# A two-layer hybrid transformer block: modulation weights in buffers of their own, a third pair begun early, bank copies asked for ahead of splits

## The chip, the cores and the metric

The kernel runs on one core of one Trainium2 chip. The core has a matrix engine (TensorE, PE in the profile; PEld is its loading of stationary operands), VectorE (DVE), ScalarE (ACT), GpSimd (POOL) and SyncE (SP). In this kernel SP starts nearly every load and store, in one queue. The engines run side by side and wait for each other by semaphores. The metric is the time of one execution on the device, in microseconds (us); lower is better.

## The reference

The reference is two layers over 1024 latent tokens and 256 context tokens, of width 1024, in 32-bit floats. Cut to what matters here:

```
def layer(x, ctx, c, c_ctx, ...):
    sh1, sc1, gt1, sh2, sc2, gt2 = split(silu(c) @ w_ada + b_ada, 6)      # modulation; the same for c_ctx
    px = (rms_norm(x, g1) * (1 + sc1) + sh1) @ w_in                       # q, k, v, f, u, gv
    mix = concat(latent_attention(q, k_all, v_all),                       # q, k: normed, rotary factors
                 fourier_mix(f), chunk_spatial_gate(u, gv)) @ w_out
    x = x + gt1 * mix
    y = rms_norm(x, g2) * (1 + sc2) + sh2
    x = x + gt2 * (square(relu(y @ w1)) @ w2)                             # w1: 1024 x 4096, w2: 4096 x 1024
```

The context tokens go through the same weights in layer 0 only, where layer 1's keys and values still need them; the output is x.

## The kernel before, in words

**Precision.** Each 32-bit operand is split into a high part, rounded by a copy on ScalarE, and the remainder, subtracted on VectorE. A product is three matmuls: high by high, high by low, low by high. So every weight block that is multiplied first passes ScalarE and VectorE.

**Stages of a layer.** Input projection, gMLP, Fourier mixing, attention in blocks of 128 queries, output mix (`mix_out`: product with `w_out`, gated residual L1323, sums of squares), second norm, MLP1, MLP2. The first 512 tokens' mix is done early, between attention units; the second 512 tokens' mix is the loop over `d` behind `split_next`, and the norm of the first half (`norm_first`) is stepped inside it.

**MLP1.** The hidden width is cut into 32 blocks of 128 columns, taken as 16 pairs `p`. Tokens (first and second 512), depth (first and second 512) and the two blocks of a pair make a 2 x 2 by 2 x 2 product, and it is done with seven products in place of eight, numbered 1 to 7, each of 12 matmuls of 128x512. In layer 0 four context products of 12 matmuls of 128x256 stand between them. The token sides (`ysum`) come from `norm_first` for products 2 and 4, and from `norm_second` for 5, 1, 7, 3, 6: the scaled x (L1464, L1465), sums (L1476, on GpSimd for c in (1, 3)), splits (L1470 on ScalarE, L1471 on VectorE). The weight sides come from `split_next`: a sum or difference of two raw blocks (L1576, in an M buffer; on GpSimd for products 2, 1, 6 in layer 0 and 2, 6 in layer 1, else on VectorE), the high part (L1578, ScalarE), the low part (L1580, VectorE), in a ring W1 of 8 buffers, that is, 4 splits. The matmuls are L1641 to L1643 (context) and L1655 to L1657.

**Behind a product.** `after_product` is called one product later. Products 2 and 4 of a pair share a PSUM bank, 5 and 3 another, 1 and 7 a third. After 2, 5 and 1 ScalarE copies the bank out (L1671). GpSimd adds copies 2 and 5 (L1673) and subtracts after product 1 (L1675); VectorE does the sums L1681, L1684, L1687 and L1691; ScalarE squares the relu (L1626, L1627); `combine` (L1618) makes five sums of the squared blocks, two of them on GpSimd, and they are stored for MLP2.

**The order of the work.** `seq` lists the products: the products 2 of pairs 0 and 1, then 4 and context for each, then 5, 1, 7, 3, 6 alternating between the two pairs, then pair after pair. `ahead_of` says how many steps of `norm_second` come ahead of a product; `split_next` is called until three splits lie ahead of the product's own, and only then are the matmuls and the pending `after_product` written. A scheduler reorders the instructions further within their dependences and buffers, so that the order on an engine isn't the code's. Buffers of one ring are given out in the order of first writing.

**Modulation.** `silu(c) @ w_ada` is a product of one vector, done on VectorE in most places. A unit (`ada_sums`, L317) is 256 columns of one of the six groups. Per step it loads 2 row blocks (256 KB) and at once multiplies each by its factor and adds it to a running sum in an SBUF buffer named pB (L328 for the first, L330 for the rest; the name pB is also that of the PSUM banks). A unit with `nj` = 2 does it for c and c_ctx: 16 instructions; with `nj` = 1 it has 8. Column sums on TensorE close it (L338, `ada_cols`). Layer 1's 20 units, 8 with `nj` = 2 and 12 with 1, load into the four M buffers that the raw sums use too, and are stepped once behind each product from pair 2 on in layer 0's MLP1, and what is left in MLP2. Layer 0's own first five units load 4 row blocks at a time into L buffers and are stepped every second step of the gMLP and projection (`GPUMP` = 2); `rope_tables` scales the rotary factors of both layers on VectorE (L636).

**MLP2** uses the same seven products with stored sums: 112 items of 12 matmuls, each with a load, a GpSimd sum of two weight blocks (L1738) and two splits (L1731, L1732; L1740, L1742), made two items ahead.

Of the kernel before, what the change touches and what calls it, by code (L numbers as in the profile page):

```python
# [11 lines left out]
F32 = mybir.dt.float32  # L12
# [27 lines left out]
GPUMP = 2  # L40
# [22 lines left out]
NBUF = {"S": 40, "L": 12, "T": 8, "M": 4, "R": 3, "W1": 8, "W2": 8, "pB": 5}  # L63
# [66 lines left out]
def hybrid_block_kernel(ctx: ExitStack, tc: tile.TileContext, a: dict, out: bass.AP):  # L130
# [186 lines left out]
    def ada_sums(l, c0, nj, mk, per):  # L317

        ac = [alloc("pB", [256], F32) for _ in range(nj)]
        for k0 in range(0, KC, per):  # L320
            w = mk(per, 256)
            load(w, a["w_ada"][l, k0 * P:(k0 + per) * P, c0:c0 + 256].rearrange("(k p) n -> p k n", p=P))
            for kk in range(per):
# [7 lines left out]
            yield None  # L331
        yield ac

    def ada_cols(l, grp, quarter, ac):
        tp = PB(2, 2)
        for j, x in enumerate(ac):
            for i in range(2):
                E.matmul(tp[:, j, i:i + 1], x[:, i * P:(i + 1) * P], ones[:, 0:1], start=True, stop=True)  # L338
        mod_cols(l, grp, quarter * 2, 2, [tp[:, j, :] for j in range(len(ac))])

    def ada_units(l, units, mk, per=4):

        prev = None
        for grp, quarter, nj in units:
            for ac in ada_sums(l, grp * D + quarter * 256, nj, mk, per):
                if ac is None:
                    yield
            if prev is not None:
                ada_cols(l, *prev)
                yield  # L350
            prev = grp, quarter, ac
        yield
        yield
        ada_cols(l, *prev)
        yield
# [261 lines left out]
    def layer(l, ys, norms, bank):  # L617
# [10 lines left out]
        def rope_tables():  # L628
# [7 lines left out]
            V.tensor_scalar_mul(grow[:, 0:4:2, :], grow[:, 0:4:2, :], -0.125)  # L636
# [842 lines left out]
        def norm_first():  # L1479

            if last:
                for k in range(KC):
                    to_tokens(0, k)
                    yield
# [3 lines left out]
            for k in range(KC):  # L1488
                x = modulated(0, res[0], k)
# [46 lines left out]
        def w1_load(p, which):  # L1536

            src = w1d[:, (p + NP * which) * P:(p + NP * which + 1) * P].rearrange("(k p) f -> p k f", p=P)
            if p % 2 and which:
                for half in range(2):  # L1540
                    t = alloc("W2", [4, P], F32)
                    load(t, src[:, 4 * half:4 * half + 4, :])
                    raws[p, which, half] = flat(t)
            else:
# [8 lines left out]
                "21": ((1, 0),), "12": ((0, 1),), "11": ((0, 0),)}  # L1553
# [453 lines left out]
```

## Time and profile before

| | |
|---|---|
| median of 3 runs | 2751.97 us (2745.11 to 2752.44) |
| the profiled execution | 2750.48 us, its span 2748.7 us |
| mean granted TensorE clock | 0.985 |
| loads of modulation weights into M | 80, of 256 KB, 3.1 us from issue to landing in the median |
| raw weight loads of MLP1 (R) | 48, of 512 KB, 4.3 us |
| VectorE's splits of weights in MLP1 (L1580, W from M) | 160, 149.6 us busy, 936 ns in the mean |
| their high parts (L1578, W from M) | 160, 98.2 us busy, 615 ns in the mean |
| idle time of ScalarE ahead of these high parts | 136.4 us, 54.8 of it for a raw sum on GpSimd |

How to read it: the profile is one execution. A row of the table by stage gives a stretch of the span in us, its length, and then for each engine the busy time with the number of instructions in brackets, the granted TensorE clock (1.00 is full speed), the share of the DMA engines and what they moved. A row of the groups gives line, engine, operation, output from inputs, shape and count, then busy us and mean ns, then the idle time just before them with what ended it. A row of the waits gives what waited for what: us in all, times, the longest. In the timeline, the first number is the start and the second the duration. Matmuls overlap, so that the busy time of one is longer than the step from one to the next.

### The profile page before, as it was taken

Reading aid. Unit: us, or ns where it says so; the run is one execution under the profiler, and the core shown is the slowest. Engines: PE = TensorE matmul, PEld = TensorE weight load, DVE = VectorE, ACT = ScalarE, POOL = GpSimd, SP = SyncE. Lnnn points to the kernel's source line nnn. Section 1 sums busy time; section 2 is a strip of 40 time slices with the busy share of each in tenths; the row PEclk is TensorE's granted clock in tenths of the full one; section 3 lists DMA queues with packets and bytes.
Section 4 is the critical chain, followed back from the end, with each engine's and each line's share of the span. In section 5 each row is a group of like instructions: output and inputs, shape, how many; then the busy total and the mean of one; then the engine's idle time right before and its main releaser. Section 6 shows DMA issues by size and latency. Waiting matters only on the chain. (4 is left out here: it accounts for less than half of the span.)

```text
span 2748.7 us, 39495 instructions
## 1 busy us (share of the span) xinstructions
PE 2613.8 (95%) x13236; PEld 2141.9 (78%) x13236; DVE 2129.4 (77%) x3663; ACT 1523.6 (55%) x3247; POOL 1064.0 (39%) x818
## 2 busy tenths in 40 slices
PE   7898899999899999999999999999999899999999
PEld 5677687787777777878878988787887688888877
DVE  7887979768898878865578684878677987766598
ACT  6535888666544334444455533889775555555443
POOL 4221745511443433334433000534314554424386
PEclk8999999999999999999999999999999999999999
DMA  8435221325054555695638521421252444486454
GB/s 280 143 110 156 79 95 36 115 70 186 29 186 159 171 159 168 212 323 169 197 118 294 163 81 57 129 92 33 88 166 87 134 157 150 164 281 202 138 170 144
DMA packets 314220, 405.08 MB, mean 147 GB/s; under 512 B 23816, under 2 KB 202400, under 8 KB 314016
## 3 DMA queue, kind: packets, MB, share of 16 engines
q1 hardware_dynamic: 308864, 393.38, 44.0%
q0 software_dynamic: 5152, 9.18, 1.2%
q8 instruction: 104, 1.70, 0.3%
q14 instruction: 100, 0.82, 0.1%
HBM read 298.92 MB, written 103.55 MB: 146 GB/s over the span
## 5 line engine op out<-in xcount | busy, mean ns | idle before, releaser
L1732 DVE TENSOR_TENSOR T<-R,T 128x512 fp32r<-128x512 f32 x224 | 186.8, 835 | 168.5 <-ACT T L1731 168.4
L1731 ACT CAST T<-R 128x512 fp32r<-128x512 f32 x224 | 138.9, 622 | 288.1 <-PE pB L197 269.7
L1142 DVE TENSOR_TENSOR T<-pB,T 128x512 fp32r<-128x512 f32 x328 | 223.3, 685 | 52.7 <-ACT T L1141 48.8
L1141 ACT CAST T<-pB 128x512 fp32r<-128x512 f32 x328 | 195.2, 600 | 72.9 <-PE pB L1139 37.2
L1655 PE MATMUL pB<-S,W 128*128 128x512 f32 x512 | 205.6, 402 | 5.6 <-ACT W L1671 3.7
L1657 PE MATMUL pB<-S,W 128*128 128x512 f32 x512 | 204.0, 398 | 4.4 <-DVE W L1580 4.1
L1656 PE MATMUL pB<-S,W 128*128 128x512 f32 x512 | 203.5, 397 | 2.3 <-DVE S L1471 2.3
L1106 DVE TENSOR_REDUCE mb<-pB 128x1 f32<-128x512 f32 x256 | 172.5, 683 | 35.4 <-PE pB L1061 34.2
L1738 POOL TENSOR_TENSOR M<-W,S 128x512 f32<-128x512 f32 x96 | 142.4, 1488 | 134.6 <-DVE W L1742 76.9
L1618 POOL TENSOR_TENSOR W<-T,T 128x512 f32<-128x512 f32 x64 | 110.5, 1746 | 185.9 <-ACT T L1627 185.9
L1122 ACT ACTIVATE L<-pB,nm 128x512 f32<-128x512 f32 x256 | 178.7, 704 | 0.1
L197 PE MATMUL pB<-W,T 128*128 128x512 f32 x448 | 175.5, 392 | 2.8 <-DVE W L1742 2.8
L196 PE MATMUL pB<-T,W 128*128 128x512 f32 x448 | 175.2, 391 | 2.3 <-ACT T L1731 2.3
L197 PE MATMUL pB<-T,W 128*128 128x512 f32 x448 | 174.8, 390 | 2.2 <-DVE T L1732 2.2
L198 PE MATMUL pB<-T,W 128*128 128x512 f32 x448 | 175.5, 392 | 1.3 <-DVE W L1742 1.1
L1139 PE MATMUL pB<-ident,L 128*128 128x128 f32 x1056 | 163.3, 277 | 14.0 <-DVE T L1142 6.4
L198 PE MATMUL pB<-W,T 128*128 128x512 f32 x448 | 174.5, 390 | 1.2 <-DVE T L1732 1.2
L196 PE MATMUL pB<-W,T 128*128 128x512 f32 x448 | 174.4, 389 | 0.0
L1578 ACT CAST W<-M 128x512 fp32r<-128x512 f32 x160 | 98.2, 615 | 136.4 <-POOL M L1576 54.8
L1655 PE MATMUL pB<-L,W 128*128 128x512 f32 x384 | 155.2, 405 | 18.5 <-ACT W L1671 9.3
L1580 DVE TENSOR_TENSOR W<-M,W 128x512 fp32r<-128x512 f32 x160 | 149.6, 936 | 28.2 <-ACT W L1578 26.7
L1139 PEld LDWEIGHTS pB<-ident,L 128*128 128x128 f32 x1056 | 128.6, 142 | 53.8 <-DVE T L1142 9.3
(340 smaller groups left out, 8266.0 us busy)
## 6 DMA issues: line engine op xcount, KB each, us to landing
R<-t SPq DMA_DIRECT2D x112, 512.0 KB, 4.0
W<-in_w_mlp SPq DMA_DIRECT2D x160, 256.0 KB, 3.4
t<-W SPq DMA_DIRECT2D x160, 256.0 KB, 2.3
S<-in_w_mlp SPq DMA_DIRECT2D x128, 256.0 KB, 5.0
R<-in_w_mlp SPq DMA_DIRECT2D x48, 512.0 KB, 4.3
M<-in_w_ada SPq DMA_DIRECT2D x80, 256.0 KB, 3.1
R<-in_w_out SPq DMA_DIRECT2D x32, 512.0 KB, 4.3
t<-T SPq DMA_DIRECT2D x64, 256.0 KB, 2.0
```

The costliest lines, as they stand in the source:

```text
L196: E.matmul(o, lh, rh, start=first, stop=False)
L197: E.matmul(o, lh, rl, start=False, stop=False)
L198: E.matmul(o, ll, rh, start=False, stop=last)
L1106: V.tensor_reduce(ma[:, k + 1:k + 2], tl[k], axis=AX.X, op=ALU.min)
L1122: A.activation(u["pa"][b][:, k * 512:(k + 1) * 512], tl[k], AF.Exp, bias=tl["nm"][:, 0:1], scale=-1.0, accum_out=u["den"][:, b, 1 + k:2 + k])
L1139: E.transpose(tp[:, b * P:(b + 1) * P], src, ident)
L1141: A.copy(ph, tp)
L1142: V.tensor_sub(pl, tp, ph)
L1655: E.matmul(o, h[:, cs], yh, start=(new and c == 0), stop=False, skip_group_check=True)
L1656: E.matmul(o, h[:, cs], yl, start=False, stop=False, skip_group_check=True)
L1657: E.matmul(o, lo[:, cs], yh, start=False, stop=(c == 3), skip_group_check=True)
L1732: V.tensor_sub(tl, src, th)
```

## The change

Six things are changed together.

1. **Buffers A.** Four buffers of 2 x 256 floats a partition hold modulation weights alone; the memory set aside for DMA descriptors is set to 8192 bytes. `ada_flow` takes the place of `ada_units`: it asks for the loads three steps ahead of the arithmetic (L351, L353 in the new code) and closes a unit after the second step of the next one (column sums L321).
2. **Where the units run.** In layer 0's own units `GPUMP` is 1. Of layer 1's, the 8 with `nj` = 2 are stepped at products 2, 1, 7 and 6 of the pairs from 3 on and finished behind MLP1; the 12 others run in MLP2, a step every second item.
3. **Rotary factors.** Layer 1's are scaled on GpSimd (L642).
4. **Three pairs.** `seq` begins with the products 2 of three pairs; product 4 of the third comes before the fives of the first two, and its other products behind theirs. The splits for the first two fives and the third pair's raw block lie in T buffers. In layer 1 `norm_first` writes the token-major copies inside its loop over k and no longer ahead of it.
5. **Copies ahead of splits.** `split_next` is called behind the matmuls and the pending `after_product`, not ahead of them.
6. **Engines.** The add after product 5 moves from GpSimd to VectorE (L1690), and so do the raw sums of the first two pairs; the squared relu of products 2 and 4 is written after both 4 and 5 are done.

Over the whole program VectorE has 3544 instructions instead of 3520, ScalarE 2794 instead of 2792, GpSimd 782 instead of 823, SP 1305 instead of 1291, and TensorE as many as before.

How instructions move, at three places. First, VectorE's queue in layer 0 after the queries' norm and rotation, where a modulation unit follows. Before (grow is the buffer of the rotary factors, L the load buffer, sil the factors):

```order
L428 SCALAR_TENSOR_TENSOR qrs_2071<-rt_2074,rr_2073 128x8
L766 TENSOR_TENSOR T_2066<-T_2066,qrs_2071 128x512
L636 TENSOR_SCALAR grow_16938<-grow_16938 128x2x64
L328 TENSOR_SCALAR pB_2144<-L_2146,sil_77 128x256
L328 TENSOR_SCALAR pB_2145<-L_2146,sil_77 128x256
L330 SCALAR_TENSOR_TENSOR pB_2144<-L_2146,sil_77,pB_2144 128x256
L330 SCALAR_TENSOR_TENSOR pB_2145<-L_2146,sil_77,pB_2145 128x256
```

After:

```order
L434 SCALAR_TENSOR_TENSOR qrs_2071<-rt_2074,rr_2073 128x8
L772 TENSOR_TENSOR T_2066<-T_2066,qrs_2071 128x512
L351 TENSOR_SCALAR pB_2224<-A_2174,sil_77 128x256
L275 TENSOR_TENSOR mod_541_2185<-pB_2180,bcol_98 128x2 x2
L353 SCALAR_TENSOR_TENSOR pB_2224<-A_2174,sil_77,pB_2224 128x256
L353 SCALAR_TENSOR_TENSOR pB_2224<-A_2194,sil_77,pB_2224 128x256
L1034 TENSOR_TENSOR L_2507<-L_2434,L_2507 128x8x64
```

The scaling of the factors is gone from the place; the unit's weights come from A; and the instruction behind it closes another unit.

Second, VectorE's queue at the last residuals of layer 0's output mix (L1323, after the change L1329, into x, named L). Before:

```order
L1323 SCALAR_TENSOR_TENSOR L_7789<-pB_8141,mod_537_2198,L_7789 128x512
L1580 TENSOR_TENSOR W_2194_8198<-M_8194,W_2193_8196 128x512
L1580 TENSOR_TENSOR W_2197_8204<-M_8200,W_2196_8202 128x512
L1580 TENSOR_TENSOR W_2204_8269<-R_8186,W_2203_8267 128x512
L1323 SCALAR_TENSOR_TENSOR L_7791<-pB_8206,mod_537_2198,L_7791 128x512
L1580 TENSOR_TENSOR W_2214_8313<-R_8186,W_2213_8311 128x512
L1323 SCALAR_TENSOR_TENSOR L_7791<-pB_8235,mod_537_2198,L_7791 128x512
L423 TENSOR_SCALAR rv_8300<-pB_8294 128x4
```

After, with layer 1's modulation (pB from A):

```order
L1329 SCALAR_TENSOR_TENSOR L_7811<-pB_8279,mod_541_2185,L_7811 128x512
L353 SCALAR_TENSOR_TENSOR pB_9483<-A_9481,sil_77,pB_9483 128x256
L353 SCALAR_TENSOR_TENSOR pB_9484<-A_9481,sil_77,pB_9484 128x256
L351 TENSOR_SCALAR pB_9749<-A_9559,sil_77 128x256
L353 SCALAR_TENSOR_TENSOR pB_9749<-A_9559,sil_77,pB_9749 128x256
L353 SCALAR_TENSOR_TENSOR pB_9749<-A_9652,sil_77,pB_9749 128x256
L1586 TENSOR_TENSOR W_2239_8385<-R_8165,W_2238_8383 128x512
L353 SCALAR_TENSOR_TENSOR pB_9749<-A_9652,sil_77,pB_9749 128x256
L353 SCALAR_TENSOR_TENSOR pB_9749<-A_9698,sil_77,pB_9749 128x256 x2
L353 SCALAR_TENSOR_TENSOR pB_9749<-A_9747,sil_77,pB_9749 128x256
L429 TENSOR_SCALAR rv_8357<-pB_8351 128x4
```

Modulation for the next layer, 40 instructions of it between the middle and the end of the mix, has moved in between the residuals, the splits (L1580, after the change L1586) and the statistics of the second half (L423, then L429).

Third, ScalarE's queue at the end of layer 1's output mix, where MLP1 begins: L1454 and then L1460 copy transposed tokens, L1671 and then L1688 copy a product's bank, L1465 and L1470, then L1471 and L1476, are the second half's norm. Before:

```order
L1454 COPY T_23223<-pB_23218 128x512
L496 ACTIVATE M_23233<-L_22707 128x512
L1671 COPY W_5821_23304<-pB_23249 128x512
L1454 COPY T_23267<-pB_23262 128x512
L424 ACTIVATE rr_23277<-rv_23276 128x4
L1578 CAST W_5824_23313<-M_23311 128x512
L1671 COPY W_5826_23329<-pB_23291 128x512
L1465 ACTIVATE L_22705<-M_23331,mod_2865_11539 128x512
L1470 CAST S_23334<-L_22705 128x512
```

After:

```order
L1584 CAST W_5847_23367<-W_5811_23188 128x512
L1688 COPY W_5838_23333<-pB_23299 128x512
L1460 COPY T_23317<-pB_23312 128x512
L1584 CAST W_5850_23385<-T_23141 128x512
L430 ACTIVATE rr_23342<-rv_23341 128x4
L1688 COPY W_5846_23365<-pB_23320 128x512
L1584 CAST W_5854_23408<-M_23406 128x512
L1688 COPY T_23383<-pB_23352 128x512
L1471 ACTIVATE L_22733<-M_23412,mod_3374_13729 128x512
L1476 CAST S_23415<-L_22733 128x512
```

Two bank copies stood ahead of the norm's first instruction, and three do now, the third in a T buffer; they stand between casts of weights (L1584).

The diff, cut to its core:

```
-GPUMP = 2
+GPUMP = 1
-NBUF = {"S": 40, "L": 12, "T": 8, "M": 4, "R": 3, "W1": 8, "W2": 8, "pB": 5}
+NBUF = {"S": 40, "L": 12, "T": 8, "M": 4, "R": 3, "W1": 8, "W2": 8, "pB": 5, "A": 4}
...
+    def ada_flow(l, units):
+
+        jobs = [(u, k) for u in units for k in range(0, KC, 2)]
+        coming = []
+
+        def fetch(n):
+            if n < len(jobs):
+                (grp, quarter, _), k = jobs[n]
+                w = alloc("A", [2, 256], F32)
+                c0 = grp * D + quarter * 256
+                load(w, a["w_ada"][l, k * P:(k + 2) * P, c0:c0 + 256].rearrange("(k p) n -> p k n", p=P))
+                coming.append(w)
+
+        for n in range(3):
+            fetch(n)
+        prev = None
+        yield
+        for n, ((grp, quarter, nj), k0) in enumerate(jobs):
+            fetch(n + 3)
+            w = coming.pop(0)
+            if k0 == 0:
+                ac = [alloc("pB", [256], F32) for _ in range(nj)]
+            for kk in range(2):
...
+            if k0 == 2 and prev is not None:
                 ada_cols(l, *prev)
+            if k0 == KC - 2:
+                prev = grp, quarter, ac
+            yield
...
-            V.tensor_scalar_mul(grow[:, 0:4:2, :], grow[:, 0:4:2, :], -0.125)
+            (G if l else V).tensor_scalar_mul(grow[:, 0:4:2, :], grow[:, 0:4:2, :], -0.125)
...
         if last:
-            seq = [(i, p) for i in (2, 4, 5, 1, 7, 3, 6) for p in range(2)]
-            seq += [(i, p) for p in range(2, NP) for i in (2, 5, 1, 4, 7, 3, 6)]
+            seq = [(i, p) for i in (2, 4) for p in range(3)]
+            rest, usual = (5, 1, 3, 7, 6), (2, 5, 1, 4, 7, 3, 6)
         else:
-            seq = [(2, 0), (2, 1)] + [(i, p) for p in range(2) for i in (4, "c22", "21", "11", "12")]
-            seq += [(i, p) for i in (5, 1, 7, 3, 6) for p in range(2)]
-            seq += [(i, p) for p in range(2, NP) for i in (2, 5, 1, 4, "c22", "21", 7, 3, "c11", "12", 6)]
-        to_split = [it for it in seq if it[0] in fops]
+            seq = [(2, 0), (2, 1), (2, 2)] + [(i, p) for p in range(2) for i in (4, "c22", "21", "11", "12")] + [(4, 2)]
+            rest, usual = (5, 1, "22", "21", 7, 3, "c11", "12", 6), (2, 5, 1, 4, "c22", "21", 7, 3, "c11", "12", 6)
+        seq += [(i, p) for i in (5, 1, 7, 3, 6) for p in range(2)]
+        seq += [(i, 2) for i in rest]
+        seq += [(i, p) for p in range(3, NP) for i in usual]
+        ahead = [(5, 0), (5, 1)]
+        to_split = [it for it in seq if it[0] in fops and it not in ahead]
...
-                (G if i in FSUM[l] else V).tensor_tensor(s, bs[0], bs[1], op[2])
+                (G if i in FSUM[l] and p > 1 else V).tensor_tensor(s, bs[0], bs[1], op[2])
...
+            if d == KC - 3:
+                w1_load(0, 0)
+                w1_load(1, 0)
+                w1_load(0, 1)
+                w1_load(2, 1, "T")
+                split_block(5, 0, "T")
             if d == KC - 2:
-                w1_load(0, 1)
                 w1_load(1, 1)
-                w1_load(0, 0)
+                split_block(5, 1, "T")
                 split_next()
+                split_next()
+            if d == KC - 1:
                 split_next()
...
-                m = fsum[p, i] = alloc("W2", [512], F32)
+                m = fsum[p, i] = alloc("T" if (i, p) == (2, 2) else "W2", [512], F32)
                 A.copy(m, o)
             if i == 5:
-                G.tensor_tensor(fsum[p, 2], fsum[p, 2], fsum[p, 5], ALU.add)
+                V.tensor_tensor(fsum[p, 2], fsum[p, 2], fsum[p, 5], ALU.add)
...
-            bg.append(ada_units(l + 1, [(g, q, 2 if g < 2 else 1) for g in range(5) for q in range(4)], M, 2))
+            bg.append(ada_flow(l + 1, [(g, q, 2) for g in range(2) for q in range(4)]))
...
-            own = to_split.index((i, p)) if (i, p) in to_split else nsplit[0] - 3
-            while nsplit[0] < min(own + 3, len(to_split)):
-                split_next()
             follow = first_product(i, p)
             while pending:
                 f, it = pending.pop(0)
                 f(*it)
+            if (i, p) in to_split:
+                own = to_split.index((i, p))
+            while nsplit[0] < min(own + 3, len(to_split)):
+                split_next()
...
-            if not last and p > 1 and i in BANK:
+            if not last and p > 2 and i in (2, 1, 7, 6):
                 pump(1)
...
+        if not last:
+            while bg:
+                pump()
+            bg.append(ada_flow(l + 1, [(g, q, 1) for g in range(2, 5) for q in range(4)]))
...
-            pump(1)
+            if n % 2 == 0:
+                pump(1)
...
-    bg.append(ada_units(0, [(g, q, 2) for g, q in units[:NDVE]], L))
+    bg.append(ada_flow(0, [(g, q, 2) for g, q in units[:NDVE]]))
...
-    nc = _bacc.Bacc("TRN2", target_bir_lowering=False, num_devices=1)
+    nc = _bacc.Bacc("TRN2", target_bir_lowering=False, num_devices=1, dynamic_dma_scratch_size=8192)
```

More of the change, by code (lines that the diff above doesn't have):

```diff
@@ L315, in ada_on_pe, with ada_cols @@
         yield
[L317 to L323, printed above, removed]
+    def ada_cols(l, grp, quarter, ac):
+        tp = PB(2, 2)
+        for j, x in enumerate(ac):
+            for i in range(2):
+                E.matmul(tp[:, j, i:i + 1], x[:, i * P:(i + 1) * P], ones[:, 0:1], start=True, stop=True)
+        mod_cols(l, grp, quarter * 2, 2, [tp[:, j, :] for j in range(len(ac))])
+    def ada_flow(l, units):
[18 more added lines that the diff above has]
+            for kk in range(2):
                 k = k0 + kk
@@ L330, in ada_sums @@
                         V.scalar_tensor_tensor(ac[j], w[:, kk, :], s, ac[j], ALU.mult, ALU.add)
[L331 to L348, printed above, removed]
+            if k0 == 2 and prev is not None:
                 ada_cols(l, *prev)
-                yield
-            prev = grp, quarter, ac
-        yield
+            if k0 == KC - 2:
+                prev = grp, quarter, ac
+            yield
         yield
@@ L1479, in norm_first @@
         def norm_first():
[L1481 to L1484, printed above, removed]
             res = []
@@ L1488, in norm_first @@
             for k in range(KC):
+                if last:
+                    to_tokens(0, k)
                 x = modulated(0, res[0], k)
@@ L1534, in layer, with w1_load @@
         raws = {}
-        def w1_load(p, which):
+        def w1_load(p, which, tag=None):
             src = w1d[:, (p + NP * which) * P:(p + NP * which + 1) * P].rearrange("(k p) f -> p k f", p=P)
-            if p % 2 and which:
+            if tag or (p % 2 and which):
                 for half in range(2):
-                    t = alloc("W2", [4, P], F32)
+                    t = alloc(tag or "W2", [4, P], F32)
                     load(t, src[:, 4 * half:4 * half + 4, :])
@@ L1669, in after_product @@
             if i in (2, 5, 1):
-                m = fsum[p, i] = alloc("W2", [512], F32)
+                m = fsum[p, i] = alloc("T" if (i, p) == (2, 2) else "W2", [512], F32)
                 A.copy(m, o)
             if i == 5:
-                G.tensor_tensor(fsum[p, 2], fsum[p, 2], fsum[p, 5], ALU.add)
+                V.tensor_tensor(fsum[p, 2], fsum[p, 2], fsum[p, 5], ALU.add)
             if i == 1:
                 G.tensor_tensor(fsum[p, 1], fsum[p, 1], fsum[p, 2], ALU.subtract)
-            if i in (4, 5) and (p, 21) not in hq and (i == 4):
-                relu2(p, 21, o)
             if i in (4, 5):
@@ L1681, in after_product @@
                     V.tensor_tensor(fsum[p, 5], fbank[p, "a"], fsum[p, 2], ALU.subtract)
+                    relu2(p, 21, fbank[p, "a"])
             if i == 7:
@@ L1830, in layer @@
                 f(*it)
+            if (i, p) in to_split:
+                own = to_split.index((i, p))
+            while nsplit[0] < min(own + 3, len(to_split)):
+                split_next()
             if follow:
                 pending.append((follow, (i, p)))
-            if i in (5, 4) and p > 0 and p + 1 < NP and (i == 5) == (p > 1):
-                w1_load(p + 1, 1)
-            if i in (1, 4) and p > 0 and p + 1 < NP and (i == 1) == (p > 1):
-                w1_load(p + 1, 0)
-            if not last and p > 1 and i in BANK:
+            if (i, p) == (3, 1):
+                w1_load(2, 1)
+                w1_load(2, 0)
+            if p > 1 and i in (5, 1) and p + 1 < NP:
+                w1_load(p + 1, 1 if i == 5 else 0)
+            if not last and p > 2 and i in (2, 1, 7, 6):
                 pump(1)
```

28 lines of the change are left out of this document (15 added, 13 removed).

## Prediction

> **What bounds the kernel now.** The head of the page says which engine sets the pace.
>
> ```profile
> span 2748.7 us, 39495 instructions
> PE 2613.8 (95%) x13236; PEld 2141.9 (78%) x13236; DVE 2129.4 (77%) x3663; ACT 1523.6 (55%) x3247; POOL 1064.0 (39%) x818
> ```
>
> TensorE (PE) is busy for 95% of the span, so time can be gained only where it stands still or runs slowly. The table by stage shows where. Layer 0: end of the output mix, its last 28 us with the first MLP1 products, MLP1, the passage to MLP2, MLP2. Then, in time order, the start, two stretches of layer 0's projections, layer 1's passage into MLP1, and its MLP1.
>
> ```profile
> core 0: us, PE busy (x) PEld busy (x) DVE busy (x) ACT busy (x) POOL busy (x), PEclk, DMA share, GB/s
> 655.00:734.00 79.00, 77.85 (x393) 64.66 (x391) 65.80 (x99) 43.17 (x79) 29.20 (x20) 1.00 0.24 77
> 734.00:762.00 28.00, 18.52 (x60) 12.66 (x59) 25.12 (x32) 15.77 (x28) 15.51 (x11) 0.88 0.24 75
> 780.00:1166.00 386.00, 361.77 (x1898) 301.40 (x1896) 329.42 (x511) 160.91 (x289) 144.46 (x93) 1.00 0.53 169
> 1166.00:1182.00 16.00, 11.65 (x48) 8.62 (x49) 10.54 (x16) 7.19 (x14) 3.47 (x2) 1.00 0.85 321
> 1182.00:1482.00 300.00, 298.66 (x1314) 244.16 (x1313) 202.63 (x287) 139.09 (x248) 127.50 (x92) 1.00 0.65 210
> ```
>
> ```profile
> 60.00:130.00 70.00, 60.03 (x277) 46.58 (x275) 58.04 (x189) 41.11 (x98) 22.55 (x18) 0.98 0.45 163
> 200.00:212.00 12.00, 5.58 (x24) 4.14 (x23) 5.98 (x17) 0.66 (x2) 0.00 (x0) 0.89 0.87 270
> 212.00:220.00 8.00, 7.85 (x25) 6.41 (x26) 8.00 (x27) 3.14 (x7) 0.00 (x0) 0.52 1.09 343
> 2112.00:2155.00 43.00, 30.92 (x100) 20.34 (x99) 39.00 (x49) 23.46 (x43) 24.09 (x14) 0.88 0.18 54
> 2155.00:2432.00 277.00, 276.94 (x1192) 224.61 (x1191) 223.44 (x247) 148.59 (x261) 132.92 (x85) 0.99 0.49 163
> ```
>
> Busy time overlaps and hides small holes, so I go by time per matmul. A 512-wide one takes 277/1192 = 0.232 us in layer 1's MLP1 and 300/1314 = 0.228 in layer 0's MLP2. The two narrow kinds in layer 0's MLP1 are priced by these rows, of which the first two are neighbours and the third is all column sums of layer 1's modulation there (one unit's eight took 0.95 us, 0.12 each).
>
> ```profile
> 849.95 0.28 PE L1641 MATMUL pB<-S,W 128*128 128x256 f32 x1
> 850.07 0.28 PE L1642 MATMUL pB<-S,W 128*128 128x256 f32 x1
> 862.18 0.95 PE L338 MATMUL pB<-ones,pB 128*128 128x1 f32 x8
> L338 PE MATMUL pB<-ones,pB 128*128 128x1 f32 x104 | 12.6, 235 | 0.0
> ```
>
> A context matmul is 0.12. By the loops the 1898 of MLP1 are about 1130 wide, 664 context and 104 column sums: 1130 x 0.232 + 664 x 0.118 + 104 x 0.12 = 262 + 78 + 12 = 353, so 33 of the 386 us are lost. What TensorE and then VectorE (DVE) waited for there:
>
> ```profile
> PE pB L1657 <- DVE W L1580: 12.6, 12, 2.3
> PE pB L1655 <- ACT W L1671: 8.0, 9, 2.2
> DVE pB L330 <- DMA M<-in_w_ada: 31.3, 19, 3.3
> DVE pB L328 <- DMA M<-in_w_ada: 14.2, 8, 3.0
> ```
>
> TensorE waits for split weights (L1580) and freed banks (L1671), and VectorE, which makes the splits, stands 45.5 us in its own queue behind modulation weights that have not landed. The same loads hold GpSimd, whose raw sums (L1576) take the same M buffers:
>
> ```profile
> POOL M L1576 <- DVE pB L330: 35.5, 13, 5.5
> ```
>
> Else the passages lose most: 28 us for 60 matmuls that need 13 (15 lost) and 43 for 100 that need 23 (20 lost); then 200 to 220.
>
> **B: MLP1 of layer 0, +32 (22 to 41).** Its VectorE groups, and the spread of the modulation instruction:
>
> ```profile
> L330 DVE SCALAR_TENSOR_TENSOR pB<-M,sil,pB 128x256 f32<-128x256 f32 x190 | 114.3, 627 | 33.0 <-DMA M<-in_w_ada 31.3
> L328 DVE TENSOR_SCALAR pB<-M,sil 128x256 f32<-128x256 f32 x26 | 18.0, 700 | 14.2 <-DMA M<-in_w_ada 14.2
> L1580 DVE TENSOR_TENSOR W<-W,W 128x512 fp32r<-128x512 f32 x14 | 16.8, 1198 | 0.0
> L330 DVE SCALAR_TENSOR_TENSOR pB<-M,sil,pB x196: 469/480/1517, 775.1 to 1157.8; 128x256 f32<-128x256 f32 x196
> ```
>
> Of 216 modulation instructions here 128 stay: 8 units of 16; the order puts 40 of those ahead of the stage, so 88 are left. Fetched three steps ahead into buffers that nothing else takes, they should not wait: a load has three products of 12 x 0.232 = 2.8 us, 8 us in all, to land, where the longest wait was 3.3. GpSimd's 35.5 us of waits for M go with them, and so does a cause of late splits. The stage then needs 262 + 78 + 44 x 0.12 = 345 us of TensorE. VectorE must keep up: without modulation it has (329.4 - 114.3 - 18.0)/14 = 14.1 us a pair (14 pairs, by the x14 above). The add after product 5 comes over from GpSimd, and its price on VectorE is bounded by neighbours of its shape, free and beside a GpSimd instruction:
>
> ```profile
> 720.43 0.68 DVE L1580 TENSOR_TENSOR W<-M,W 128x512 fp32r<-128x512 f32 x1
> 721.25 1.79 POOL L1476 TENSOR_TENSOR M<-L,L 128x512 f32<-128x512 f32 x1 [1.30 <-DVE W L1580]
> 721.80 1.79 DVE L1580 TENSOR_TENSOR W<-M,W 128x512 fp32r<-128x512 f32 x1
> L1673 POOL TENSOR_TENSOR W<-W,W x32: 1261/1726/1797, 729.6 to 2419.4; 128x512 f32<-128x512 f32 x32
> ```
>
> So 0.7 to 1.8 for it (1.2 taken, as for the subtraction with both inputs in W). With one unit a pair, 16 x 0.627 = 10.0, a pair costs VectorE 14.1 + 1.2 + 10.0 = 25.3, against 84 x 0.232 + 48 x 0.118 + 8 x 0.12 = 26.1 on TensorE. That is 97%, in the six pairs or so that still carry a unit; I add 9 us there for waits that such a load leaves: 354, a gain of 32. With none of it the gain is 41; with 3 us a pair, 22.
>
> Here a rule speaks against the change. The Trainium skill, page "SBUF — State Buffer", section "Who interferes with whom", says that a VectorE instruction with two SBUF inputs contends with a GpSimd one that reads SBUF, and that the later of the two is blocked until the other ends. The modulation instruction reads its weights and its running sum from SBUF, and so does the add that comes over; had each of them to sit out a GpSimd instruction, each would cost about 1.5, VectorE would set the pace of the six pairs, and the time would be 2836 (last rival). The trace agrees that this happens, 0.68 against 1.79 above and a longest of 1.517, but not that it is the rule: the median is 0.48, the mean 0.627.
>
> **A: 200 to 220, +9 (6 to 12).**
>
> ```profile
> 202.63 0.23 DVE L636 TENSOR_SCALAR grow<-grow 128x128 f32<-128x128 f32 x1 [6.56 <-DMA grow<-in_q_norm_g]
> 206.25 0.62 DVE L328 TENSOR_SCALAR pB<-L,sil 128x256 f32<-128x256 f32 x2 [3.39 <-DMA L<-in_w_ada]
> 212.15 1.84 PE L338 MATMUL pB<-ones,pB 128*128 128x1 f32 x8 [6.57 <-DVE pB L330]
> ```
>
> VectorE waits 6.56 us for the next layer's rotary factors, then 3.39 for modulation weights, and TensorE stands 6.57 for the sums; in the 8 us after that its granted clock is 0.52, another 8 x 0.48 = 3.8: 10.4 lost. By the order shown with the change, the scaling has left VectorE ahead of this unit (it stands on GpSimd, idle there: 0.00), and the weights, now in A, were asked for three steps earlier. Both waits go; I keep 1.4 for what is then late, the column sums' own unit. Six is the wait alone, 12 all of it and a quicker start behind it.
>
> **F: 60 to 130, -2.5 (-6 to +1).** GPUMP 1 moves layer 0's units forward: four loads more and 12 to 14 modulation instructions stand earlier in SP's and VectorE's queues.
>
> ```profile
> 118.93 6.97 SPq L177 DMA_DIRECT2D R<-in_w_in  x2
> ```
>
> 14 x 0.48 = 6.7 us meet VectorE's 12 idle of 70, so most is covered; behind the loads on SP is this input weight, for which TensorE's next groups wait. Half of the 6 is taken.
>
> **C0: into layer 0's MLP1, -2 (-8 to +4).** Two products of a third pair fill 24 x 0.228 = 5.5 us of the 15 lost. But VectorE gets more ahead of it: by the order, modulation (L351, L353 of the new code) now stands among the mix's last residuals and splits, ahead of the statistics on which the second half's norm hangs. Over the whole mix end it is 40 instructions: 40 x 0.48 = 19 us against 13.2 + 2.9 = 16 idle in 655 to 762, 3 over. Six raw sums of the first two pairs come from GpSimd too, 0.7 to 1.8 each, some 7, of which I charge 4.5 since they are made ahead. 5.5 - 3 - 4.5 = -2. If modulation runs at 0.627 and nothing is hidden it is -8 or worse; if the idle time takes it all, +4.
>
> **D: passage to MLP2, +3 (0 to 6).** 48 matmuls in 16 us need 11, 5 are lost. Modulation ended at 1157.8; now it ends six pairs earlier and the last pair's sums are not behind it.
>
> **E: MLP2 of layer 0, -8 (-16 to -2).** 12 units come here: 96 x 0.627 = 60 us on VectorE's 97 idle of 300, so covered, at 88%; their 48 column sums take 48 x 0.12 = 6 us of TensorE, not covered, since it is 99.5% busy; 2 more for collisions. With a sixth of the 60 uncovered it is -16.
>
> **C1: into layer 1's MLP1, +9 (0 to 16).** Of its 43 us 20 are lost; these are the chain's pieces and the bank wait.
>
> ```profile
> 2145.99 1.71 POOL M L1576
> 2147.72 4.19 DMA R<-in_w_mlp
> 2152.05 1.31 POOL M L1576
> PE pB L1655 <- ACT W L1671: 5.0, 2, 3.0
> ```
>
> A raw sum holds the buffer that a weight load waits for, which holds the next sum. By ScalarE's order there, three bank copies of the products 2 stand ahead of the second norm's work, where there were two: TensorE has a third pair to go on with while the norm runs, and a copy is now asked for ahead of the splits that follow it. Most of the 5.0 goes, the third pair's products fill 5.5, the first pairs' sums on VectorE shorten the chain by about 2; 3.5 are given back in new holes, as VectorE has 4 idle of 43. Zero is all handed on to VectorE.
>
> **Sum.** 9 - 2.5 - 2 + 32 + 3 - 8 + 9 = 40.5. From this execution's 2750.5 (1.5 under the median of 2752.0) that is 2710. The deferred relu and the third pair's later loads cost nothing: they lie in stages where ScalarE and SP have idle time.
>
> **Rivals.** A measurement of this kernel tells 0.3%, 8 us, from no change.
> - *The split chain binds on* (0.20). The waits for L1671 and those for L1580 that no DMA caused stay, as ScalarE's casts and the ring of four splits are unchanged; then B is 12, about half of TensorE's waits: 2730. For it: 97% on VectorE. Against: layer 1's MLP1, the same ring, runs at 0.232 with VectorE at 81%.
> - *The mix end pays* (0.08): 40 x 0.627 - 16 = 9, and six sums at 1.8 = 11; C0 is 5.5 - 20 = -14: 2722.
> - *The passages nearly close* (0.10): C0 +12 and C1 +18 of 15 and 20 lost: 2687.
> - *The loads aren't early* (0.05), so that the change doesn't do what it says: SP has one queue, and an A load stands behind weight loads and stores. 88/216 of the 45.5 us of waits, 18, stays: 2728.
> - *Slower* (0.05): with VectorE full, GpSimd's reads lengthen modulation, one mechanism in two stages. At m us each it adds 88(m - 0.627) in MLP1 and 96m - 97 in MLP2 where that is positive. At 1.198, the mean of the W subtraction, that is 50 + 18 = 68: 2778; at 1.5, the longest, 77 + 47 = 124 and some 2 for the adds: 2836. It eats the gain from m = 1.05. Against it: a mean of 0.627 beside a GpSimd that had 41 more instructions.
>
> **How the numbers follow.** My case has 0.50, the rest 0.02 for what I have not seen. Range 2678 to 2736: the ends of seven terms drawn together as independent (17 us each way), the closing passages below, the first two rivals and late loads above; outside lie the slower case, and tails of the rest. Slower by over 0.3%: 0.05. Within 0.3%: 0.05, the split chain together with a dear mix end. Faster: 0.90.
>
> **What would show it.** No wait of the modulation on a DMA in MLP1, and the stage near 354 us; 200 to 212 without the 6.57 wait; MLP2 about 308 with VectorE near 88%; TensorE's idle in layer 1's passage down by 9. I am wrong if MLP1 keeps over 15 us of waits for splits, if modulation's mean passes 1 us, or if the mix end grows.

## The result, and the profile after

The changed kernel takes 2720.77 us (median of 4 runs, 2718.94 to 2723.11) against 2751.09 for the kernel before (4 runs). The ratio is 0.9894, interval 0.9881 to 0.9907: faster by 30 us, or 1.1%. The forecast was 2710 with 2678 to 2736 as range, so sign and range held; of 40 us foretold 30 came. That the sum comes within 10 us is in part luck: terms A with F, C0 and C1 came out 21 us lower than foretold, and B, D, E and a gain in layer 1 that nobody foretold 11 higher. The profiled execution took 2719.93 us.

The head of the page of the changed kernel:

```profile
span 2718.2 us, 39508 instructions
PE 2604.6 (96%) x13236; PEld 2146.8 (79%) x13236; DVE 2174.0 (80%) x3705; ACT 1527.2 (56%) x3248; POOL 1018.5 (37%) x777
```

Where did the time come from? A matmul group that the change left alone can be looked up in both traces: its first and last start tell how far ahead the new kernel is. Before (groups by line and tiles: layer 0's MLP2, then layer 1's):

```profile
L196 PE MATMUL pB<-T,W x448: 387/389/504, 1166.6 to 1482.4; 128*128 128x512 f32 x150
L196 PE MATMUL pB<-W,T x448: 387/389/398, 2432.0 to 2743.2; 128*128 128x512 f32 x150
```

After:

```profile
L196 PE MATMUL pB<-T,W x448: 388/389/477, 1134.7 to 1450.5; 128*128 128x512 f32 x150
L196 PE MATMUL pB<-W,T x448: 387/389/398, 2401.8 to 2712.9; 128*128 128x512 f32 x150
```

Layer 0's MLP2 begins 31.9 us earlier and ends 31.9 earlier, layer 1's begins only 30.2 earlier. Doing the same for every matmul of an unchanged line (matched by line, tiles and count) gives a running lead, and its steps stand beside the terms of the prediction:

| stretch (time in the trace before) | lead at its ends, us | gained | foretold |
|---|---|---|---|
| start to 645 (A and F) | 0 to -0.3 | -0.3 | +6.5 |
| mix end and first products, 645 to 780 (C0) | -0.3 to -4.0 | -3.7 | -2 |
| MLP1 of layer 0, 780 to 1166 (B) | -4.0 to 31.0 | +35.0 | +32 |
| passage to MLP2 (D) | 31.0 to 36.8 | +5.8 | +3 |
| MLP2 of layer 0 (E) | 36.8 to 31.8 | -5.0 | -8 |
| layer 1 up to its MLP1 | 31.8 to 34.1 | +2.3 | 0 |
| passage into layer 1's MLP1 (C1) | 34.1 to 30.2 | -3.9 | +9 |

(The lead can be read as it stands at 780: there both kernels have done 18 products of 12 matmuls and all 8 context products of the first two pairs, and begin the third pair's context.)

The table by stage of the changed kernel, in its own times: two stretches of the start, mix end with the first products, MLP1, passage, MLP2, then layer 1's passage and MLP1.

```profile
core 0: us, PE busy (x) PEld busy (x) DVE busy (x) ACT busy (x) POOL busy (x), PEclk, DMA share, GB/s
200.00:212.00 12.00, 10.54 (x52) 8.62 (x50) 4.06 (x10) 1.82 (x4) 0.54 (x1) 1.00 0.58 176
212.00:220.00 8.00, 7.99 (x32) 6.27 (x33) 7.21 (x23) 4.12 (x9) 0.00 (x0) 0.79 0.70 209
700.00:760.00 60.00, 53.52 (x270) 44.78 (x269) 53.83 (x86) 30.61 (x56) 21.17 (x12) 0.94 0.11 36
760.00:1134.00 374.00, 366.35 (x1929) 311.19 (x1928) 319.01 (x456) 175.82 (x313) 134.33 (x87) 1.00 0.53 172
1151.00:1451.00 300.00, 298.87 (x1338) 245.47 (x1338) 269.63 (x351) 137.85 (x246) 139.37 (x93) 1.00 0.69 225
2075.00:2125.00 50.00, 39.11 (x139) 28.75 (x138) 41.22 (x59) 29.31 (x52) 18.45 (x10) 0.86 0.17 48
2125.00:2402.00 277.00, 271.98 (x1164) 219.92 (x1163) 217.60 (x257) 148.34 (x256) 112.46 (x71) 0.99 0.49 164
```

Read against the rows before, MLP1 is the changed place: TensorE is now busy for 366 of 374 us, and MLP2 carries 351 VectorE instructions instead of 287 with TensorE as busy as it was. What TensorE waited for in 760 to 1134, and what the modulation waited for over the whole program:

```profile
PE pB L1674 <- DVE W L1586: 3.7, 2, 2.0
PE pB L1660 <- DVE W L1586: 2.4, 2, 2.2
PE pB L1673 <- DVE L L1477: 1.3, 1, 1.3
PE pB L1672 <- ACT W L1584: 0.3, 1, 0.3
```

```profile
L353 DVE SCALAR_TENSOR_TENSOR pB<-A,sil,pB x266: 397/481/1531, 89.4 to 1315.2; 128x256 f32<-128x256 f32 x133
  DMA A<-in_w_ada: 1.2, 2
```

The 23.8 us of TensorE's waits in MLP1 are 7.7, of which 2.4 lie behind 780, and L353 waits 1.2 us for its loads (L351, the other modulation instruction, 1.0) where modulation waited 45.5 in that stage alone. The median of L353, 481 ns, is what it was.

How much modulation was in the stage? The groups of VectorE in 760 to 1134:

```profile
L353 DVE SCALAR_TENSOR_TENSOR pB<-A,sil,pB 128x256 f32<-128x256 f32 x112 | 66.3, 599 | 2.0
L351 DVE TENSOR_SCALAR pB<-A,sil 128x256 f32<-128x256 f32 x16 | 9.7, 608 | 0.0
```

That is 128 instructions, not the 88 of the prediction. 40 of the stage's own had moved ahead into the mix end, as foretold, but 40 of the 96 that the change gives to MLP2 had moved ahead into MLP1 in their turn, all before 1060; MLP2 was left with 56.

### The profile page after: what moved, and what is told of

It is laid out like the page before. It is cut to its first block, busy times and chain, and to the rows that moved or that the text cites. A ratio compares the mean times of both kernels' runs of the same rounds, so it can differ in the third digit from the quotient of the medians.

```text
span 2718.2 us, 39508 instructions
## 1 busy us (share of the span) xinstructions
PE 2604.6 (96%) x13236; PEld 2146.8 (79%) x13236; DVE 2174.0 (80%) x3705; ACT 1527.2 (56%) x3248; POOL 1018.5 (37%) x777
## 4 chain that ended last, share of the span: by engine, by line
PE 76%; DVE 14%; ACT 4%; issue 3%; DMA 2%; POOL 1%; SPq 0%; DVEq 0%; ACTq 0%; POOLq 0%
PE pB L196 12%; PE pB L198 12%; PE pB L197 12%; PE pB L1672 7%; PE pB L1674 7%; PE pB L1673 7%; PE pB L1145 4%; PE pB L1158 2%; PE pB L1159 2%; PE pB L1066 2%; PE pB L1067 2%; PE pB L1980 1%; PE pB L1979 1%; PE pB L1978 1%; DVE pB L353 1%
## 5 line engine op out<-in xcount | busy, mean ns | idle before, releaser
L1748 DVE TENSOR_TENSOR T<-R,T 128x512 fp32r<-128x512 f32 x224 | 198.0, 885 | 94.4 <-ACT T L1747 94.4
L1674 PE MATMUL pB<-S,W 128*128 128x512 f32 x496 | 197.2, 398 | 3.4 <-DVE W L1586 3.4
L1673 PE MATMUL pB<-S,W 128*128 128x512 f32 x496 | 197.0, 397 | 0.7 <-DVE S L1477 0.7
L1672 PE MATMUL pB<-S,W 128*128 128x512 f32 x496 | 197.6, 398 | 0.0
L1758 DVE TENSOR_TENSOR W<-M,W 128x512 fp32r<-128x512 f32 x160 | 182.7, 1142 | 0.0
L1586 DVE TENSOR_TENSOR W<-M,W 128x512 fp32r<-128x512 f32 x156 | 135.4, 870 | 33.6 <-ACT W L1584 33.1
```

What stands on the lines that cost most here:

```text
L1672: E.matmul(o, h[:, cs], yh, start=(new and c == 0), stop=False, skip_group_check=True)
L1673: E.matmul(o, h[:, cs], yl, start=False, stop=False, skip_group_check=True)
L1674: E.matmul(o, lo[:, cs], yh, start=False, stop=(c == 3), skip_group_check=True)
L1748: V.tensor_sub(tl, src, th)
L1758: V.tensor_sub(sl, s, sh)
```

## The experiments

My theory went into them as the prediction had it: MLP1's loss was VectorE standing in its queue behind modulation loads (waits). The first rival is that the number of modulation instructions counted (quantity); the second, that the rest of the change did it. Each ratio is against the kernel before on the same chip; differences in us are read as above, along the trace of the changed kernel (plus is later), unless another is named.

**Own buffers alone**, on the kernel before:

```
-NBUF = {..., "pB": 5}
+NBUF = {..., "pB": 5, "A": 4}
-bg.append(ada_units(l + 1, [...], M, 2))
+bg.append(ada_units(l + 1, [...], lambda *s: alloc("A", s, F32), 2))
```

(and the descriptor memory at 8192). 

> The kernel before with one thing changed: layer 1's modulation weights load into the four buffers A, all 20 units still stepped behind MLP1's products. Theory of waits (the 33 us lost in layer 0's MLP1 were VectorE standing in its queue behind modulation loads): the stage gains 25 to 33 us, the mix end gives 2 to 8 back because modulation moves into it, total about 2725 (2718 to 2732). Theory of quantity (what counted is that 216 modulation instructions became 88): only the 37 that move ahead count, 2745. Theory of the rest (third pair, copies ahead of splits, the add on VectorE): 2751, within 3.

Measured 2741.73, ratio 0.9962 (0.9949 to 0.9976). In its trace no modulation waits for a load in MLP1 any more, and yet TensorE still waits (780 to 1134):

```profile
PE pB L1657 <- DVE W L1580: 4.4, 9, 1.5
PE pB L1655 <- ACT W L1671: 3.3, 4, 1.3
PE pB L1655 <- ACT W L1578: 2.8, 5, 1.0
PE pB L1643 <- DVE W L1580: 1.6, 2, 1.2
```

The stage gains 17.5 us and the passage behind it 4.5; the mix end loses 15, of which 2 come back by 780. Neither theory has it: the waits were at most half of the 35.0, for with 40 instructions moved ahead into the mix end the stage also had 184 modulation instructions instead of 215.

**One buffer, asked for at use:** `"A": 1`, `fetch(n)` in place of `fetch(n + 3)`, and none fetched ahead.

> The changed kernel with one buffer A in place of four and each load asked for at its use, so that a load starts only behind the arithmetic of the step before. Theory of waits: each step makes VectorE stand about 3 us; some 22 to 32 steps in layer 0's MLP1 bring back 15 to 30 us there, layer 0's start loses 3 to 8, MLP2 covers its own: 2738 to 2757. Theory of quantity: the instructions are as few as in the changed kernel, so 2721 to 2727.

Measured 2768.23, ratio 1.006 (1.0044 to 1.0077), slower than the kernel before. VectorE's wait for modulation loads in 780 to 1200, and TensorE's at the start (195 to 250), where the sums are late:

```profile
DVE pB L351 <- DMA A<-in_w_ada: 28.1, 16, 3.9
DVE pB L349 <- DMA A<-in_w_ada: 4.9, 6, 2.3
```

```profile
PE pB L321 <- DVE pB L351: 20.7, 2, 11.1
```

From 752, behind the mix end, MLP1 and its passage lose 26 us (21 of them from 784 on) with 33 us of waits; the start loses 28. The mix end *gains* 5, with 25 modulation instructions in it, not 40. The number of instructions is that of the changed kernel (in MLP1 140 against 128), so the waits alone undo about half of the 40.8 us that MLP1 and its passage had gained.

**All 20 units in MLP1, through A:** the three edits that moved units to MLP2 undone.

> The changed kernel with all 20 units of layer 1 stepped behind each main product of MLP1 from pair 2 on, as before, but through A. Theory of waits: VectorE has room (14.1 + 1.2 + 9.7 = 25 us a pair against 26), so MLP1 loses 5 to 8 us, most of it 60 column sums, MLP2 gains 5 back: 2719 to 2726. Theory of quantity: MLP1 loses 15 or more, 2731 to 2741.

Measured 2743.14, ratio 0.9968 (0.9958 to 0.9978). MLP1 loses 22.5 us, MLP2 gives 4.8 back: here quantity has it, with hardly a wait for loads (some 6 of the 22.5 are 48 more column sums on TensorE, at 0.12 each). The rows of 40 us show how. This kernel:

```profile
860.00:900.00 40.00, 35.84 (x185) 29.04 (x185) 39.61 (x75) 18.04 (x34) 12.83 (x8) 1.00 0.48 157
900.00:940.00 40.00, 35.93 (x192) 29.54 (x190) 38.31 (x64) 12.03 (x23) 15.41 (x10) 1.00 0.71 224
1060.00:1100.00 40.00, 40.00 (x215) 34.27 (x215) 31.29 (x41) 19.36 (x35) 17.55 (x11) 1.00 0.41 135
```

The changed kernel in the same stretches:

```profile
860.00:900.00 40.00, 40.00 (x224) 34.66 (x223) 36.85 (x59) 16.81 (x30) 13.86 (x9) 1.00 0.47 150
900.00:940.00 40.00, 40.00 (x209) 33.88 (x208) 37.99 (x60) 19.42 (x35) 12.91 (x8) 1.00 0.48 162
1060.00:1100.00 40.00, 40.00 (x210) 34.01 (x209) 30.06 (x34) 19.39 (x35) 16.08 (x11) 1.00 0.40 133
```

Where VectorE is busy 39.6 of 40 us, TensorE is busy 35.8 and does 185 matmuls instead of 224 (not quite of the same kinds); where it is at 31, nothing is lost. Both theories fit into one: what counts is VectorE's *queue time*, work and waits for loads together. Before, MLP1 had 329.4 us of work and 45.5 of waits for loads in 386 us, 97%. Own buffers took the waits, moving units took work; with the waits gone and the units kept (this kernel and the first) the queue stays full. How full is too full the runs don't say: the changed kernel loses nothing with VectorE at 38.0 (900 to 940 above), and the kernel with own buffers alone does at 37.7:

```profile
860.00:900.00 40.00, 36.89 (x185) 29.73 (x184) 37.73 (x60) 18.41 (x35) 15.05 (x10) 1.00 0.43 141
```

What else decides is not shown.

**The add after product 5 back on GpSimd:** `V.tensor_tensor(fsum[p, 2], ...)` is `G.` again.

> The changed kernel with the add after product 5 back on GpSimd. Theory of waits: the add hides on either engine, 2719 to 2724. Theory of the rest: the add's place in the chain from product 5 to the sums decides part of the gain, so both MLP1 stages lose, 3 to 6 us each: 2727 to 2733.

Measured 2729.41, ratio 0.9918 (0.99 to 0.9937). Of the 8 us, 4 lie in the first 645 us, where both kernels have the same instructions in the same order (more on this at the end). MLP1 of layer 0 loses 3.2, layer 1's passage 0.6. So the add's place is worth some 4 us: less than the rest-theory said, more than mine. On VectorE it takes 0.68 each of 30 times, where GpSimd took 1.73:

```profile
L1690 DVE TENSOR_TENSOR W<-W,W x30: 677/680/687, 747.8 to 2389.5; 128x512 f32<-128x512 f32 x30
```

**Two pairs in layer 1:** `seq` for the last layer as before, `(i, p) for i in (2, 4) for p in range(2)`, with its `ahead_of` and loads.

> The changed kernel with the order of before in layer 1's MLP1 alone: two pairs begin early, not three, and the third pair's raw block is loaded at its usual place. Layer 1's passage into MLP1 lost 4 to 5 us by the change instead of gaining 9. Theory that the third pair does it (its sums, splits and copies lie in VectorE's and ScalarE's queues just where these are full): the passage gets 4 to 9 back, 2712 to 2717. Theory that it is something else in that passage (raw sums on VectorE, splits asked for later): the third pair's 24 matmuls no longer fill 5.5 us, so the passage loses up to 5 more, 2721 to 2726. Layer 0 stays as it is in both.

Measured 2720.31, ratio 0.9874 (0.9855 to 0.9894). Layer 1's passage gets 5.6 us back, so in this layer the third pair costs more than it fills. (The median looks unmoved; the first 645 us of its profiled execution, the longest of the four, are 6 us longer in identical order, and this chip ran the kernel before at 2754.27.)

**Raw sums of the first pairs on GpSimd:** `and p > 1` taken out.

> The changed kernel with the raw sums of the first pairs for products 2, 1, 6 (layer 0) and 2, 6 (layer 1) back on GpSimd. Theory that these sums on VectorE cost the passages: layer 1 gets 2 to 5 back and layer 0 as much, 2711 to 2717. Theory that they shorten the chain: 2 to 5 lost in each, 2725 to 2731.

Measured 2724.9, ratio 0.9892 (0.9871 to 0.9912). Layer 1's passage gets 2.3 back; layer 0's loses 0.4 (2.0 from 690 on, after a gain of 1.6 at about 660). So these sums on VectorE cost a little in layer 1 and nothing in layer 0.

**Splits ahead of copies:** the `while nsplit[0] < ...` loop moved ahead of `first_product`, as before.

> The changed kernel with splits asked for ahead of the matmuls and the bank copies, as before. Theory that asking later makes the splits late in layer 1's passage: it gets 4 to 8 back, while layer 0's MLP1 keeps its time within 3: 2712 to 2718. Theory that copies ahead of splits are part of the gain: each MLP1 loses 3 to 8 by waits for copied banks, 2726 to 2736.

Measured 2718.95, ratio 0.9872 (0.9854 to 0.9889). Layer 0 gets 5.2 back between 645 and 795, 3.7 of it at the first products, and layer 1's passage 3.0; the end of MLP1 loses 1.2. So one of the change's parts, the one in its name, works against it; by totals alone it would be unclear, the intervals overlap.

**Modulation held behind MLP1's start:** a no-sync order between the first modulation instruction of layer 1 and the last VectorE instruction written ahead of it.

> The changed kernel with the first modulation instruction of layer 1 held, on VectorE, behind what the program wrote ahead of it, so that none moves into layer 0's output mix. With one buffer, where none moved either, the mix end was 5 us shorter. Theory that VectorE's time is what counts in mix and MLP1 alike: the mix end gains 5, and MLP1 with 128 instructions in place of 88 loses about 40 x 0.6 = 24 us of VectorE's time, of which it has some 15 to spare in its first pairs: 5 to 10 lost, total 2720 to 2726. Theory that moving them ahead is a plain loss: 2714 to 2717.

Measured 2721.87, ratio 0.9883 (0.9866 to 0.99). The mix end, first in this kernel, then in the changed one, and what TensorE waited for in the latter between 640 and 800:

```profile
700.00:740.00 40.00, 39.36 (x223) 33.87 (x222) 31.29 (x47) 19.62 (x37) 14.13 (x7) 1.00 0.07 27
```

```profile
700.00:740.00 40.00, 36.10 (x197) 31.27 (x196) 33.83 (x60) 17.27 (x32) 12.55 (x6) 0.91 0.14 47
```

```profile
PE pB L522 <- POOL T L503: 3.9, 1, 3.9
PE pB L475 <- DVE M L471: 2.9, 2, 2.1
```

The mix end is 9.7 us shorter, for the statistics (L475, L522) no longer wait behind modulation, and MLP1 pays only 1.7. (Up to 1.5 of the 9.7 may be chance: three of the kernels above that leave this modulation where it was gain as much at about 660.) But the hold was also on the units of MLP2, so that none of their 96 instructions moved ahead into MLP1, and MLP2 lost 7.6. That was a fault of the experiment, mended below, but it tells the other side: moving ahead cost 9.7 where it went into the mix end and was worth 7.6 where it went into MLP1's later part, in which TensorE lost nothing by it.

**Units every second step** (`GPUMP = 2`) and **rotary factors on VectorE** (`V.tensor_scalar_mul(grow, ...)`), one execution each.

> The changed kernel with GPUMP back at 2: layer 0's own units are stepped every second step, and in SP's queue the loads of keys and values stand ahead of the units' last eleven loads, not among them. Theory of SP's queue (the stretch 200 to 220 gained 6 and 220 to 240 gave 5 back since loads of keys, values and queries wait behind modulation loads that wait for a free buffer A): 220 to 240 loses 3 to 5 less, 60 to 130 loses 2 to 4 less, and 200 to 220 keeps its gain. Theory that the units must be early: the column sums' wait of 3 to 6 us at 200 to 220 is back and the rest is as it was. Either total lies within the 4 us by which executions of this kernel differ, so the stretches decide.

> The changed kernel with layer 1's rotary factors scaled on VectorE again. Theory that this wait was the heart of term A: VectorE stands some 6 us at about 200 for the factors' load, and the column sums' matmuls wait 3 to 6 us again. Theory that the prefetch did it: VectorE's queue has the unit's arithmetic behind it either way, and TensorE waits less than 2 us at that place.

Measured 2717.05 and 2722.14. TensorE's waits in 195 to 262, of the changed kernel, then with factors on VectorE, then with every second step:

```profile
PE pB L1026 <- ACT S L1018: 3.1, 2, 2.9
PE pB L321 <- DVE pB L353: 1.5, 1, 1.5
```

```profile
PE pB L1026 <- ACT S L1018: 3.2, 2, 3.0
PE pB L321 <- DVE pB L353: 1.8, 1, 1.8
```

```profile
PE pB L1026 <- ACT S L1018: 3.4, 1, 3.4
```

The rotary factors make no difference: VectorE stands 6.5 us for them again and TensorE notices 0.3. With every second step, 195 to 255 is 6.5 us shorter and the sums' wait is gone, so the theory that the units must be early falls. The theory of SP's queue is borne out in part. SP, in the changed kernel and then with every second step:

```profile
213.56 7.23 SPq L177 DMA_DIRECT2D A<-in_w_ada  x5
220.84 2.84 SPq L177 DMA_DIRECT2D M<-q  x6
```

```profile
213.82 3.49 SPq L177 DMA_DIRECT2D A<-in_w_ada  x4
217.44 3.87 SPq L177 DMA_DIRECT2D M<-q  x6
```

Five modulation loads hold SP for 7.23 us, and the queries behind them start at 220.84 against 217.44; in the kernel before it was 216.04. But 220 to 239 still gives 4.2 back (6.7 in the changed kernel), and 60 to 130 is not better (2.0 later at 195), so the larger part of the 6.5, some 4, is in 195 to 220.

**Combined:** splits ahead of copies, two pairs in layer 1, and the hold for the first eight units only; then the same with `GPUMP = 2`.

> The changed kernel with three of its parts undone or mended: splits asked for ahead of bank copies, as before; two pairs early in layer 1; the first modulation instruction for layer 1 held behind what the program wrote ahead of it in layer 0's MLP1 (not in MLP2). By the single runs: layer 0's passage 5 less, layer 1's 6, the mix end 10 less and MLP1 2 more, together 17 to 19: 2698 to 2708. If the parts pay for the same idle time, as VectorE's full queue would have it, only the larger ones count: 2708 to 2714.

> The same with GPUMP at 2. By the theory of SP's queue 4 to 8 us less than the combined kernel, by the other 2 to 6 more.

Measured 2710.22, ratio 0.9849 (0.9832 to 0.9865), and 2703.8, ratio 0.9832 (0.9813 to 0.9851). The mix end gains 9.7, layer 0's passage 3.3, layer 1's 8.7, and MLP1 loses 4.3, with 3.3 us of a longer first part on top: not quite additive, as VectorE's queue again has more in MLP1. Every second step takes 6.4 us off the median (intervals overlap), inside the 4 to 8 that SP's queue was given. Both are faster than both kernels.

## Why the prediction was right, and where it wasn't

- **What bounds it, and B.** Right in place and size (35.0 for 32), but not as counted. One step that failed is "so 88 are left": 128 were done in the stage, and it gained all the same. The other is the weight of "they should not wait", with the moved units only as what lets VectorE keep up: own buffers alone bring 17.5, and with all units left in MLP1 22.5 of the stage's gain is lost. The step that held is the count of VectorE's time in a pair that carries a unit (25.3 of 26.1 us, 97%): in 860 to 1020 it is busy for 94% and TensorE for all of the time. So the 9 us added for a nearly full engine were too many; the stage took 351 us, not 354, with 64 column sums instead of 44. The add came out at 0.68, not 1.2.
- **The rule on SBUF.** The Trainium skill, page "SBUF — State Buffer", section "Who interferes with whom", says that VectorE instructions with two SBUF inputs contend with GpSimd's reads. The trace agrees, and shows which of them pay. Of the changed kernel's 266 L353, 42 began while a GpSimd instruction was running; 35 of these took 1.10 to 1.53 us and ended 0.28 us behind it, as here, and the other 7 began within 0.06 us of its end. The remaining 224, 26 of them with a GpSimd instruction that began later, took 0.40 to 0.49.

```profile
949.75 1.40 POOL L1582 TENSOR_TENSOR M<-W,R 128x512 f32<-128x512 f32 x1 [3.43 <-DVE W L1586]
950.04 1.40 DVE L353 SCALAR_TENSOR_TENSOR pB<-A,sil,pB 128x256 f32<-128x256 f32 x1
```

  So of these two it is the one that comes second that is held, 35 of 266 here, with GpSimd busy for 134 of MLP1's 374 us. The add was never lengthened (677 to 687 ns): in 7 of its 32 times a GpSimd instruction began while it ran, and the one time that it began inside one, of 4.07 us, it was not held. The slower rival, which rested on every one being held, did not happen.
- **A.** Foretold 9 (with F 6.5 together); -0.3 in this execution. By the running lead F lost 3.6 for the 2.5 foretold, 195 to 220 gained 7.1, 220 to 239 gave 6.7 back, and 3.9 came in again up to 645. The step of A that failed is "Both waits go; I keep 1.4 for what is then late". The wait of 6.57 went down to 1.5, but what came back up to 239 is for the most part a wait for the casts L1018 (3.1 us; 0.7 for L1012 before) and the slower clock behind it (0.68 in 230 to 240, 1.00 before). The casts start no earlier than they did; before, then after:

```profile
229.82 0.62 ACT L1012 CAST S<-L 128x512 fp32r<-128x512 f32 x1
```

```profile
230.70 0.62 ACT L1018 CAST S<-L 128x512 fp32r<-128x512 f32 x1
```

  With every second step they start at 226.93. The step also named a cause that was none, the rotary factors. The granted clock in 212 to 220 went from 0.52 to 0.79, and it is 1.00 with every second step. The Trainium skill, page "TensorE: Matmul & The Clock Gate", Part 1, has the clock at half after an idle window of about 3.4 us; the trace agrees, with 6.57 us of standing ahead of the 0.52. In the changed kernel the 0.79 came behind 1.5 us of standing between column sums; no run here takes that apart.
- **C0.** Foretold -2, -3.7 by the trace, by two errors that cancel in part. Modulation moved ahead costs up to 9.7 at the mix end where I priced 3: I set 19 us of it against 16 idle, and did not see that the idle time lies elsewhere than the statistics that then wait. (By the running lead the mix end up to 735 loses 8.8.) In turn 735 to 780 gains 5.1, where the third pair and the raw sums together were set at 1; TensorE's wait for copied banks went from 5.0 (L1671, 734 to 762 before) to 2.6 (L1688, 690 to 760 after).
- **D and E** came within 3 us. Column sums, 48 x 0.12 = 6, are enough for all that MLP2 lost; of the 96 modulation instructions priced there, 56 came.
- **C1.** Foretold +9, measured -3.9, the term furthest off. The step that failed: "a copy is now asked for ahead of the splits ... Most of the 5.0 goes". The row it rests on, 5.0 for L1671, is of layer 0's passage (734 to 762). In layer 1's (2112 to 2155) TensorE waited for no bank copy; its longest wait was for the split's cast, and that wait grew; before, then after (2060 to 2140):

```profile
PE pB L1655 <- ACT W L1578: 3.7, 3, 2.8
```

```profile
PE pB L1672 <- ACT W L1584: 9.4, 4, 3.1
```

  So asking for copies ahead of splits had nothing to win here. In the new order a raw sum (L1582) stands on VectorE behind y splits and sums, its cast (L1584) follows, and then TensorE goes on:

```profile
2093.62 0.68 DVE L1582 TENSOR_TENSOR M<-R,R 128x512 f32<-128x512 f32 x1
2095.53 0.62 ACT L1584 CAST W<-M 128x512 fp32r<-128x512 f32 x1
2096.21 0.50 PE L1672 MATMUL pB<-L,W 128*128 128x512 f32 x1 [3.05 <-ACT W L1584]
```

  The runs price it: third pair 5.6, order of copies and splits 3.0, raw sums 2.3, overlapping. My lower end, "zero is all handed on to VectorE", named the mechanism and was still too kind.
- **The rivals.** Neither the split chain (2730) nor late loads (2728) held; "the mix end pays" was true in its place (8.8 lost up to 735) and partly hidden by what followed.

What stays open: the 2.3 us gained in layer 1's attention, where no line was changed, how full VectorE's queue may be before TensorE loses time, and how much of the first part's 6.5 us by every second step is SP's queue.

## What to carry to other kernels

When an engine's queue is full, add up its work and the waits inside the queue, and ask what brings the *sum* below the pace of the bounding engine; taking away one of the two may show little. Prefetched side work has no dependence left that keeps it back; here it moved into the stage ahead twice. Look in the trace where it went: it paid where the bounding engine lost nothing by it, and cost where that stage had a chain of its own, and there it is worth holding. Before a wait is priced, see that its row is of the stretch in question. A change of many parts that gains can hold parts that lose: here undoing two, holding a third and slowing a fourth brought another 17 us.

## What the runs showed that I had not expected

The first 645 us differ by up to 6 us between executions with the same instructions in the same order: against the kernel before they lie 0.3 to 6.5 us later in nine profiled executions with four buffers and `GPUMP` at 1 (mean 3.6; one of them has the factors on VectorE), 2.4 earlier in the mean of two with 2. The changed kernel's own profile is the luckiest of the nine, so A and F together are rather -4 than -0.3, and a difference of a few us is better read along the trace than from totals.
